# Transposing the gated sum, the convolution's operands and the compressed probabilities by VectorE blocks and DMAs in a decoder trunk

## The chip, the cores and the metric

The kernel runs on one core of a Trainium2 chip. A core has five engines with instruction queues of their own, which run in order: TensorE (PE in the profile: matmuls and transposes against an identity; PEld is its weight load), VectorE (DVE), ScalarE (ACT), GpSimd (POOL) and SyncE (SP). DMAs are issued from these queues and carried out by 16 DMA engines. The metric is the device time of one launch in microseconds (us), as a median of several runs; lower is better.

## The reference

Two layers of a hybrid decoder trunk on 256 tokens of width 1024, all in float32. Each layer is a half-step SwiGLU (2816 wide), a token mixer and a second SwiGLU, each between two RMSNorms:

```python
for l in range(2):
    x = x + 0.5 * rms_norm(swiglu(rms_norm(x, ...)), ...)
    x = x + rms_norm(token_mixer(rms_norm(x, ...), mem, ...), ...)
    x = x + 0.5 * rms_norm(swiglu(rms_norm(x, ...)), ...)
```

The mixer projects its input h once and splits the columns among three branches, whose outputs are gated and summed:

```python
u, bg, cg, q, kv, nsa_g, q_mem, merge_g = split(h @ w_in)
y_conv = bg * short_conv(cg * u, conv_w)               # 3 taps along the tokens, 512 channels
y_nsa  = nsa_attention(...)                            # compressed + selected blocks + window, 8 heads
y_mem  = cross_attention(q_mem, mem)                   # 4 heads, 256 memory tokens
merged = g_conv * (y_conv @ w_br_conv) + g_nsa * (y_nsa @ w_br_nsa) + g_mem * (y_mem @ w_br_mem)
return merged @ w_out
```

The compressed part of the attention has 15 compressed keys per group; its softmax gives 16 columns (one of them masked) for each of 8 heads, 128 columns for 128 tokens.

## The kernel before, in words

**Tiles.** The 256 tokens are two tiles of 128, t = 0 and 1, each a stream of work (`stream`, line 1451) that goes through the sub-layers of both layers in order. Every float32 matrix is split into a high and a low part of a reduced type (fp32r), and a product is three matmuls: high by high, high by low, low by high (`mm3`, line 395). Weights come from HBM by SP's queue into `raw`; `split_unit` (line 327) makes `whi` on ScalarE (line 333) and `wlo` on VectorE (line 334). One such unit serves both streams.

**Transposes.** A matmul contracts over partitions, so an operand that a stage leaves with tokens on partitions has to be turned before the next product. The kernel has two ways. `transpose4` (line 438) multiplies four 128x128 blocks by an identity on TensorE, into one of two PSUM banks `pt`; the users then read PSUM. `turn` (line 447) has VectorE transpose 32x32 blocks within each quarter of the partitions (tile `blocks`, line 451) and then four DMAs from GpSimd's queue carry the blocks to their partitions (tile `moved`, line 457), each DMA from a quarter of 32 partitions. For this, the source is written with its columns dealt out four apart (`lanes_in` reads with a stride of four floats, `lanes_out` writes runs of 32). `turn` is used for the SwiGLU gates, the memory, its keys and the probabilities of the selected, window and memory attention; `transpose4` for the rest.

**Order.** The program is written in steps: each `yield 0` of a stream is one step, usually six matmuls of 512 columns. The two streams take turns, stream 0 at most three steps ahead (`LEAD`), and other work (attention, compression, memory) runs in up to four lanes between the steps (`background`). `later(n, f)` puts f off by n steps: CONV, BS, PC, HALF and SECOND are such delays. Weight splits are written up to four steps ahead of their use (`AHEAD`). SP's queue keeps the written order; on the other engines a planner of the framework, which simulates the instructions with a cost model, fixes the order before the run, with priority by the written order. Small tiles of 520 columns come from one pool of eight (`TBUFS`, `ttile`), wide ones of 1024 from another (`gtile`), those of at most 128 columns from a third (`sp`).

**Around the change.** In `mixer` (line 1361) the projections u, C and B are made one after another. `conv_part` (line 1281) makes v = C * u, turns it, and applies the three taps with tokens along the free dimension, into `cT`; `conv_out` (line 1309) turns B into `bs`, multiplies and splits into `yconv`, which the first branch product reads. `cmp_attention` (line 1178) makes the compressed probabilities `pc` with a threefold copy, turns them with four 96-row transposes (line 1204) and splits them into `phc`. The branches follow in the order convolution, memory, sparse attention; each adds its gated half to `merged` (line 1438), and the two finished halves are turned by `transpose_half`, the first HALF = 5 steps after its last add, the second at step SECOND = 2 of the output product (`between`, line 1444). The output product (`output`, line 639) takes a pair of half products per step for k = 0 to 4; k from 4 up reads the second half.

## Time and profile before

| | |
|---|---|
| median of 3 runs | 1190.25 us (1189.96 to 1190.47) |
| the profiled execution | 1190.01 us, its span 1188.3 us |
| TensorE busy | 1177.2 us, 99%, 5777 matmuls, clock 0.999 of full |
| VectorE busy | 891.7 us, 75% |
| ScalarE busy | 755.9 us, 64% |
| GpSimd busy | 177.2 us, 15% |
| turns by blocks and DMAs | 44, with 176 DMAs of line 457, 4.3 us to landing in the median |
| transposes by `transpose4` (line 441) | 224 in all: x 96, qs 32, merged 32, qms 16, v 16, bs 16, kvs 8, kd 8 |
| transposes of pc (line 1204) | 16 |

The profile is one execution, followed by the hardware. In rows of groups a line reads: line of the kernel, engine, operation, tile written and tiles read, shapes, how many; then busy us, mean ns of one, and the engine's idle time ahead of them with what ended it. In rows by one line: min/median/max ns, first and last start. In a timeline: start, us, engine, line, operation. Matmuls are pipelined, so a matmul's record is longer than the time to the next one's start. The first layer's mixer runs from about 198 to 424 us, the second layer's from about 784 to 1010 us.

### The profile page before, as it was taken

To read this page: it belongs to the slowest core of one execution; us is meant where nothing else is said; L and a number is where in the kernel's file an instruction comes from. 1 tells how busy PE (TensorE), PEld (TensorE's weight loads), DVE (VectorE), ACT (ScalarE), POOL (GpSimd) and SP (SyncE) were. 2 spreads that over 40 slices of the span, in tenths; PEclk is the share of its full clock that TensorE was granted. 3 is DMA by queue.
4 is the path that set the end of the run, shared out by engine and by line. 5 is a ranking of instruction groups with operands and counts; after the bars stand their busy time and mean duration, and the time that the engine had idled before them with its cause. 6 is when DMAs were issued, how large, how long until landed. Compare 5 with 4: busy or idle time off the path is not lost.

```text
span 1188.3 us, 16619 instructions
## 1 busy us (share of the span) xinstructions
PE 1177.2 (99%) x5777; PEld 1032.5 (87%) x5777; DVE 891.7 (75%) x1130; ACT 755.9 (64%) x1217; POOL 177.2 (15%) x333
## 2 busy tenths in 40 slices
PE   9999999999999999999999999999999999999997
PEld 7888888888988888888888888889888888888886
DVE  6867757798998786676577677588899977767753
ACT  6655836888885565555465565469889655655541
POOL 4001301411120020011011011014012200110100
PEclk9999999999999999999999999999999999999999
DMA  7787875776678767777767678757767687587771
GB/s 258 253 256 240 276 261 154 228 240 192 194 231 216 247 185 221 222 235 230 228 184 230 215 229 270 240 141 242 232 178 229 198 231 229 178 250 213 234 223 63
DMA packets 133764, 260.64 MB, mean 219 GB/s; under 512 B 15694, under 2 KB 36848, under 8 KB 133680
## 3 DMA queue, kind: packets, MB, share of 16 engines
q1 hardware_dynamic: 124048, 235.11, 63.7%
q0 software_dynamic: 9600, 24.47, 7.6%
q8 instruction: 45, 0.74, 0.3%
q14 instruction: 39, 0.32, 0.1%
q10 hardware_dynamic: 32, 0.01, 0.0%
HBM read 235.42 MB, written 2.10 MB: 200 GB/s over the span
## 4 chain that ended last, share of the span: by engine, by line
PE 95%; ACT 2%; DVE 1%; issue 1%; DMA 0%; POOL 0%; SPq 0%; DVEq 0%; POOLq 0%; ACTq 0%
PE acc L410 35%; PE acc L396 9%; PE acc L397 9%; PE acc L398 9%; PE y L398 7%; PE y L396 7%; PE y L397 7%; PE pt L441 2%; PE br L396 2%; PE br L398 2%; PE br L397 2%; ACT whi L333 1%; PE s L1070 1%; DVE wlo L334 0%; PE om L1268 0%
## 5 line engine op out<-in xcount | busy, mean ns | idle before, releaser
L334 DVE TENSOR_TENSOR wlo<-raw,whi 128x1024 fp32r<-128x1024 f32 (+2 forms) x441 | 529.0, 1211 | 186.0 <-ACT whi L333 182.0
L333 ACT CAST whi<-raw 128x1024 fp32r<-128x1024 f32 (+2 forms) x441 | 452.6, 1040 | 255.2 <-PE acc L410 116.1
L457 POOL DMA_DIRECT2D moved<-blocks x176 | 95.8, 563 | 644.6 <-DVE blocks L451 368.9
L410 PE MATMUL acc<-wlo,hThi 128*128 128x512 f32 x640 | 191.6, 380 | 0.0
L410 PE MATMUL acc<-whi,hTlo 128*128 128x512 f32 x640 | 191.4, 380 | 0.0
L410 PE MATMUL acc<-whi,hThi 128*128 128x512 f32 x640 | 191.4, 381 | 0.0
L396 PE MATMUL acc<-whi,hThi 128*128 128x512 f32 (+1 forms) x480 | 182.8, 381 | 0.0
L397 PE MATMUL acc<-wlo,hThi 128*128 128x512 f32 (+1 forms) x480 | 179.3, 374 | 0.3 <-DVE wlo L334 0.2
L398 PE MATMUL acc<-whi,hTlo 128*128 128x512 f32 (+1 forms) x480 | 178.9, 373 | 0.0
L410 PEld LDWEIGHTS acc<-whi,hTlo 128*128 128x128 f32 x640 | 121.2, 189 | 17.3 <-DVE hTlo L513 0.4
L410 PEld LDWEIGHTS acc<-wlo,hThi 128*128 128x128 f32 x640 | 121.1, 189 | 17.0 <-DVE wlo L334 0.3
L410 PEld LDWEIGHTS acc<-whi,hThi 128*128 128x128 f32 x640 | 120.7, 189 | 16.6
L396 PE MATMUL y<-whi,turnhi 128*128 128x512 f32 x352 | 133.8, 380 | 0.0
L397 PE MATMUL y<-wlo,turnhi 128*128 128x512 f32 x352 | 133.7, 380 | 0.0
L398 PE MATMUL y<-whi,turnlo 128*128 128x512 f32 x352 | 133.7, 380 | 0.0
L398 PEld LDWEIGHTS acc<-whi,hTlo 128*128 128x128 f32 x480 | 90.9, 189 | 11.6
L397 PEld LDWEIGHTS acc<-wlo,hThi 128*128 128x128 f32 x480 | 91.1, 190 | 10.9 <-DVE wlo L334 0.9
L396 PEld LDWEIGHTS acc<-whi,hThi 128*128 128x128 f32 x480 | 91.1, 190 | 10.3
L398 PEld LDWEIGHTS y<-whi,turnlo 128*128 128x128 f32 x352 | 66.7, 189 | 9.2
L397 PEld LDWEIGHTS y<-wlo,turnhi 128*128 128x128 f32 x352 | 66.7, 189 | 9.2
L396 PEld LDWEIGHTS y<-whi,turnhi 128*128 128x128 f32 x352 | 66.7, 189 | 9.2
L475 DVE TENSOR_TENSOR turnlo<-moved,turnhi 128x1024 fp32r<-128x1024 f32 (+1 forms) x42 | 49.1, 1168 | 26.8 <-ACT turnhi L474 26.4
(307 smaller groups left out, 1449.6 us busy)
## 6 DMA issues: line engine op xcount, KB each, us to landing
raw<-in_ffn_w_in_dram SPq DMA_DIRECT2D x159, 512.0 KB, 4.7
raw<-in_w_mix_in_dram SPq DMA_DIRECT2D x96, 512.0 KB, 4.5
raw<-in_ffn_w_out_dram SPq DMA_DIRECT2D x88, 512.0 KB, 4.6
moved<-blocks POOLq DMA_DIRECT2D x144, 128.0 KB, 4.3
raw<-in_ffn_w_in_dram SPq DMA_DIRECT2D x34, 256.0 KB, 4.0
raw<-in_w_mem_kv_dram SPq DMA_DIRECT2D x16, 512.0 KB, 4.6
raw<-in_w_mix_out_dram SPq DMA_DIRECT2D x16, 512.0 KB, 4.9
raw<-in_cmp_k_w_dram SPq DMA_DIRECT2D x8, 512.0 KB, 4.6
```

The lines of the kernel that those rows point to most:

```text
L333: pinned(nc.scalar.copy(hi[:, c0:c1], raw[:, c0:c1]))
L334: pinned(nc.vector.tensor_sub(lo[:, c0:c1], raw[:, c0:c1], f32(hi[:, c0:c1])))
L396: nc.tensor.matmul(ps, lhsT=xh, rhs=wh, start=start, stop=False, skip_group_check=skip)
L397: nc.tensor.matmul(ps, lhsT=xh, rhs=wl, start=False, stop=False, skip_group_check=skip)
L398: nc.tensor.matmul(ps, lhsT=xl, rhs=wh, start=False, stop=stop, skip_group_check=skip)
L410: pinned(nc.tensor.matmul(ps[j][:, :n], lhsT=hT[x2][:, k], rhs=moving(w, j * n, n), start=(k == 0 and i == 0), stop=(k == 7 and i == 2)))
L441: pinned(nc.tensor.transpose(pt[:, j * P:(j + 1) * P], src[:, c0 + j * P:c0 + (j + 1) * P], ident))
L457: nc.gpsimd.dma_start(moved[0][:, q * f:(q + 1) * f], blocks[q * 32:(q + 1) * 32, :n].rearrange("j (p f) -> j p f", p=4))
L475: nc.vector.tensor_sub(lv, mv, f32(hv))
L1070: nc.tensor.matmul(s3[:, i], lhsT=QT[:, g * 2 + u, i], rhs=pairs(KT[j][:, var * 2 + g], 0, 256), start=(i == 0 and j == 0), stop=(i == 1 a ...
```

## The change

Four operands of the mixer no longer go through TensorE.

- v and bs are written dealt out four apart and turned by `turn` in place of `transpose4`, and the following instructions read the moved tile or `vT` in SBUF in place of PSUM. The scale of u and C is applied in one (`r[4]`, with `r[0]` for B in place of `r[1]`), so v is a plain product. The delays CONV and BS go from 7 and 4 to 9 and 9.
- pc is written once, without its copies, as 128 columns in a tile of the third pool; VectorE transposes its blocks, four DMAs bring the 32 columns of each pair of heads to partitions 0 to 31, and two ScalarE copies (one of them to partitions 64 to 95) and VectorE's subtraction make the three parts of `phc`. The delay PC of 3 after ATT_B becomes AWAY = 1 and PMOVED = 7.
- The last add of each half of merged writes `laned`, dealt out, which is turned by `turn`; the split comes 11 (first half) or 8 (second half) steps later, or at steps 0 and 4 of the output product if these come first. HALF and SECOND are no longer used.

```diff
--- before.py
+++ after.py
@@ -57,10 +57,12 @@
 LANES = 4
 NORM_B, NORM_C = 1, 1
 AWAY, SPLIT, RETURN = 1, 11, 6
+PMOVED = 7
+MOVED = {0: 11, 1: 8}
 MSTEP, MWAIT = (5, 11), 3
 ABREAST = 6
 SECOND_HALF = 1
-CONV, BS, CMP, ZC, QS_0, QS_1, QM, PC, YM = 7, 4, 6, 2, 2, 6, 2, 3, 1
+CONV, BS, CMP, ZC, QS_0, QS_1, QM, PC, YM = 9, 9, 6, 2, 2, 6, 2, 3, 1
 ATT_A, ATT_B, ATT_C, ATT_D, ATT_T = 1, 3, 2, 6, 8
 EARLY, RAMP, SCALES, STAGED, SETUP = 6, 10, 5, 8, 30
 DRAINED = 4
@@ -1194,17 +1196,21 @@
         sm = sp.tile([P, 8], F32, name="smc")
         nc.vector.tensor_reduce(sm, sc, axis=AX.X, op=OP.add)
         r = recip_gate(sm, 8, view(S["gt"][t], 0, [[3, 8]]))
-        pc = ttile("pc")
-        nc.vector.tensor_tensor(view(pc, 0, [[96, 4], [16, 2], [1, 16]]), view(sc, 0, [[16, 4], [64, 2], [1, 16]]),
+        pc = sp.tile([P, P], F32, name="pc")
+        nc.vector.tensor_tensor(view(pc, 0, [[32, 4], [16, 2], [1, 16]]), view(sc, 0, [[16, 4], [64, 2], [1, 16]]),
                                 view(r, 0, [[1, 4], [4, 2], [0, 16]]), op=OP.mult)
-        nc.scalar.copy(view(pc, 32, [[96, 4], [32, 2], [1, 32]]), view(pc, 0, [[96, 4], [0, 2], [1, 32]]))
-        yield ATT_B + PC
-        pt = tbank()
-        for i in range(4):
-            nc.tensor.transpose(pt[0:96, i * P:(i + 1) * P], pc[:, i * 96:(i + 1) * 96], ident)
+        blocks = sp.tile([P, P], F32, name="pb")
+        nc.vector.transpose(blocks, pc)
+        yield AWAY
+        moved = ttile("pmoved")
+        for q in range(4):
+            nc.gpsimd.dma_start(view(moved[0:32], q * 32, [[P, 4], [1, 32]]),
+                                view(blocks[q * 32:(q + 1) * 32], 0, [[32, 4], [1, 32]]))
+        yield PMOVED
         ph = ttile("phc", F32R)
-        nc.scalar.copy(ph[0:96, :512], pt[0:96])
-        nc.vector.tensor_sub(ph[32:64, :512], pt[32:64], f32(ph[32:64, :512]))
+        nc.scalar.copy(ph[0:32, :512], moved[0:32, :512])
+        nc.scalar.copy(ph[64:96, :512], moved[0:32, :512])
+        nc.vector.tensor_sub(ph[32:64, :512], moved[0:32, :512], f32(ph[0:32, :512]))
         yield ATT_D
         o = bank("oc")
         nc.tensor.matmul(o, lhsT=S["VST"][0:96], rhs=moving(ph[0:96], 0, 512), start=True, stop=True)
@@ -1281,44 +1287,42 @@
     def conv_part(t, l, u_s, c_ps, r):
         S = shared[l]
         v = ttile("v")
-        nc.vector.scalar_tensor_tensor(v[:, :512], c_ps, r[0], u_s[:, :512], op0=OP.mult, op1=OP.mult)
+        nc.vector.tensor_tensor(lanes_out(v, 0, [[P, 4]]), lanes_in(u_s, 0, 512), lanes_in(c_ps, 0, 512), op=OP.mult)
         cT = ttile("cT")
 
-        def turn():
-            pt = transpose4(v, 0)
+        def shifted(mv):
             vT = tp.tile([P, 4, 130], F32, name="vT", tag="tmp")
             if t == 0:
                 nc.gpsimd.memset(vT[:, :, 0:2], 0.0)
                 S["carry"] = sp.tile([P, 4, 2], F32, name="carry", bufs=1)
             else:
                 nc.gpsimd.tensor_copy(vT[:, :, 0:2], S["carry"])
-            nc.scalar.copy(vT[:, :, 2:130], pt.rearrange("p (c s) -> p c s", c=4))
+            nc.scalar.copy(view(vT, 2, [[130, 4], [32, 4], [1, 32]]), mv)
             if t == 0:
                 nc.gpsimd.tensor_copy(S["carry"], vT[:, :, 128:130])
             base = l * 48 + 32
             for c in range(4):
                 dst = cT[:, c * P:(c + 1) * P]
                 w = [convT[:, base + 4 * i + c:base + 4 * i + c + 1] for i in range(3)]
-                nc.scalar.activation(dst, pt[:, c * P:(c + 1) * P], AF.Copy, scale=w[2])
+                nc.scalar.activation(dst, vT[:, c, 2:130], AF.Copy, scale=w[2])
                 nc.vector.scalar_tensor_tensor(dst, vT[:, c, 1:129], w[1], dst, op0=OP.mult, op1=OP.add)
                 nc.vector.scalar_tensor_tensor(dst, vT[:, c, 0:128], w[0], dst, op0=OP.mult, op1=OP.add)
 
-        later(CONV, turn)
+        turn(v, 512, shifted, CONV)
         return cT
 
     def conv_out(cT, b_ps, r, put):
         bs = ttile("bs")
-        nc.scalar.activation(bs[:, :512], b_ps, AF.Copy, scale=r[1])
-
-        def turn():
-            pt = transpose4(bs, 0)
-            nc.vector.tensor_tensor(cT[:, :512], cT[:, :512], pt, op=OP.mult)
+        nc.scalar.activation(lanes_out(bs, 0, [[P, 4]]), lanes_in(b_ps, 0, 512), AF.Copy, scale=r[0])
+
+        def gated(mv):
+            nc.vector.tensor_tensor(quarters(cT[:, :512], 4), quarters(cT[:, :512], 4), mv, op=OP.mult)
             y = gtile("yconv", F32R)
             nc.scalar.copy(y[:, 0:512], cT[:, :512])
             nc.vector.tensor_sub(y[:, 512:1024], cT[:, :512], f32(y[:, 0:512]))
             put(y)
 
-        later(BS, turn)
+        turn(bs, 512, gated, BS)
 
     def branch(yT, name, l, n0):
         ps = bank("br")
@@ -1392,18 +1396,34 @@
         mem_query(t, l, ps, r)
         ps = yield from columns(0)
         u_s = ttile("us")
-        nc.scalar.activation(u_s[:, :512], ps, AF.Copy, scale=r[0])
+        nc.scalar.activation(u_s[:, :512], ps, AF.Copy, scale=r[4])
         ps = yield from columns(1024)
         cT = conv_part(t, l, u_s, ps, r)
         ps = yield from columns(512)
         made = []
         conv_out(cT, ps, r, made.append)
         merged = [ttile(f"merged{n}") for n in range(2)]
+        last_half = [None, None]
         mh, ml = gtile("mThi", F32R), gtile("mTlo", F32R)
 
         def transpose_half(n):
             sl = slice(n * 512, (n + 1) * 512)
             evac_split(mh[:, sl], ml[:, sl], transpose4(merged[n], 0))
+
+        placed = [False, False]
+
+        def move_half(n, laned, wait):
+            def place(mv):
+                if placed[n]:
+                    return
+                placed[n] = True
+                sl = slice(n * 512, (n + 1) * 512)
+                hv, lv = quarters(mh[:, sl], 4), quarters(ml[:, sl], 4)
+                nc.scalar.copy(hv, mv)
+                nc.vector.tensor_sub(lv, mv, f32(hv))
+
+            moved = turn(laned, 512, place, wait)
+            return lambda: place(turned_view(moved[0], 512))
 
         for b in ORDER:
             name = ("w_branch_conv", "w_branch_nsa", "w_branch_mem")[b]
@@ -1435,14 +1455,24 @@
                     nc.vector.scalar_tensor_tensor(dst, th[:, :512], 1.0, pb, op0=OP.add, op1=OP.mult)
                 else:
                     nc.vector.scalar_tensor_tensor(th[:, :512], th[:, :512], 1.0, pb, op0=OP.add, op1=OP.mult)
-                    nc.vector.tensor_add(dst, dst, th[:, :512])
-                if b == ORDER[2] and n == 0:
+                    if b == ORDER[2] and n in MOVED:
+                        laned = ttile("laned")
+                        nc.vector.tensor_tensor(lanes_out(laned, 0, [[P, 4]]), lanes_in(merged[n], 0, 512),
+                                                lanes_in(th, 0, 512), op=OP.add)
+                        last_half[n] = move_half(n, laned, MOVED[n])
+                    else:
+                        nc.vector.tensor_add(dst, dst, th[:, :512])
+                if b == ORDER[2] and n == 0 and 0 not in MOVED:
                     later(HALF, lambda: transpose_half(0))
         mT = tokens_last(mh, ml)
         y = [bank("y0"), bank("y1")]
 
         def between(k):
-            if k == SECOND:
+            if k == 0 and 0 in MOVED:
+                last_half[0]()
+            if k == 4 and 1 in MOVED:
+                last_half[1]()
+            if k == SECOND and 1 not in MOVED:
                 transpose_half(1)
 
         yield from output(y, "w_mix_out", l, 8, lambda k: (mT[0][:, k], mT[1][:, k]), between)
```

`turn`, `lanes_in`, `lanes_out`, `turned_view` and `quarters` are those of the kernel before.

## The prediction

> **What bounds the kernel now.** I read the page first, for the busy shares and the chain of work that ended last.
>
> ```profile
> span 1188.3 us, 16619 instructions
> PE 1177.2 (99%) x5777; PEld 1032.5 (87%) x5777; DVE 891.7 (75%) x1130; ACT 755.9 (64%) x1217; POOL 177.2 (15%) x333
> ...
> PE 95%; ACT 2%; DVE 1%; issue 1%; DMA 0%; POOL 0%; SPq 0%; DVEq 0%; POOLq 0%; ACTq 0%
> ```
>
> TensorE sets the end almost everywhere, so work taken from it is worth its issue time, as long as no other engine makes it wait instead. Next came the windows of the first mixer, because a share of 75% for VectorE is a mean over unlike stages. A row gives the stretch and its length, then the busy us (and instructions) of PE, PEld, DVE, ACT and POOL, the clock, the DMA share and GB/s.
>
> ```profile
> 278.00:294.00 16.00, 16.00 (x92) 14.24 (x91) 15.27 (x34) 12.85 (x26) 2.66 (x7) 1.00 0.70 233
> 294.00:310.00 16.00, 16.00 (x92) 14.39 (x91) 15.06 (x26) 12.27 (x32) 2.18 (x4) 1.00 0.52 144
> 310.00:326.00 16.00, 16.00 (x89) 14.42 (x89) 15.01 (x23) 16.00 (x41) 2.16 (x4) 1.00 0.77 230
> 326.00:342.00 16.00, 16.00 (x80) 14.04 (x79) 15.55 (x22) 13.19 (x27) 4.34 (x8) 1.00 0.80 252
> 342.00:358.00 16.00, 16.00 (x80) 13.94 (x79) 15.61 (x25) 13.22 (x29) 2.16 (x4) 1.00 0.73 214
> 358.00:374.00 16.00, 16.00 (x76) 13.93 (x75) 13.31 (x14) 8.58 (x12) 2.17 (x4) 1.00 0.79 212
> ...
> 390.00:406.00 16.00, 16.00 (x80) 14.05 (x79) 12.97 (x15) 9.57 (x12) 0.00 (x0) 1.00 0.80 260
> ```
>
> From 278 to 358 us, where the convolution and the compressed attention run, VectorE is busy 76.5 of 80 us: it is nearly a second bound. From 358 on it has about 3 us free in 16. The third view counts, for the weights' low parts (tile wlo), the VectorE splits begun and the TensorE matmuls that used them, from the start of the span to a given time (columns PE, PEld, DVE). Each split serves four matmuls (441 splits, 1760 uses), so splits less a quarter of the uses says how far VectorE is ahead.
>
> ```profile
> 0.00:252.00 252.00, 128.74 (x388) 71.10 (x388) 117.66 (x100) 1.00 0.76 240
> ...
> 0.00:342.00 342.00, 170.75 (x500) 92.17 (x501) 151.40 (x128) 1.00 0.74 233
> 0.00:358.00 358.00, 178.66 (x521) 96.04 (x521) 158.66 (x134) 1.00 0.74 232
> ...
> 0.00:408.00 408.00, 206.05 (x594) 109.87 (x594) 183.85 (x155) 1.00 0.75 232
> ```
>
> The lead is 100 - 388/4 = 3.0 splits at 252 us, 3.0 at 342, 3.75 at 358 and 6.5 at 408. At 251 us TensorE does wait for a split, as the waits of TensorE and the chain show:
>
> ```profile
> PE z L1111 <- DVE wlo L334: 1.0, 2, 0.6
> ```
> ```profile
> 250.99 0.30 PE z L1111
> ```
>
> So in the convolution's stage VectorE has about one split in hand, and in the stage of the gated sum (from about 382 us) three more.
>
> **What TensorE is rid of.** Five groups of four transposes per token tile and layer: v, bs, pc and the two halves of merged.
>
> ```profile
> L441 PE MATMUL pt<-ident,merged x32: 272/273/273, 389.0 to 997.0; 128*128 128x128 f32 x32
> ...
> L441 PE MATMUL pt<-ident,v x16: 271/273/275, 288.5 to 883.0; 128*128 128x128 f32 x16
> ...
> L441 PE MATMUL pt<-ident,bs x16: 272/273/273, 297.4 to 892.8; 128*128 128x128 f32 x16
> ```
> ```profile
> L1204 PE MATMUL pt<-ident,pc x16: 272/273/273, 286.1 to 878.9; 128*96 128x128 f32 x16
> ```
> ```profile
> 388.76 0.38 PE L398 MATMUL acc<-whi,hTlo 128*128 128x512 f32 x1
> 388.97 0.60 PE L441 MATMUL pt<-ident,merged 128*128 128x128 f32 x4
> 389.33 0.46 PE L396 MATMUL acc<-whi,hThi 128*128 128x512 f32 x1
> 389.63 0.38 PE L397 MATMUL acc<-wlo,hThi 128*128 128x512 f32 x1
> ```
>
> The 273 ns of a record is latency; what counts is start to start. A wide matmul takes 0.215 us to the next start (388.76 to 388.97). From 388.76 to 389.63 stand two wide matmuls and a group in 0.87 us, so a group costs 0.44 us. 80 transposes are 20 groups: 8.8 us. Per layer (two token tiles) that is 2.64 us in the convolution's stage and 1.76 us in the gated sum's. Nothing else leaves TensorE.
>
> **What VectorE gets.** The rows nearest to the new instructions:
>
> ```profile
> L451 DVE STREAM_TRANSPOSE blocks<-wide 128x1024 f32<-128x1024 f32 x16 | 19.8, 1239 | 0.0
> ...
> L1438 DVE TENSOR_TENSOR merged<-merged,gth 128x512 f32<-128x512 f32 x16 | 10.9, 684 | 0.3
> ...
> L451 DVE STREAM_TRANSPOSE blocks<-wide 128x768 f32<-128x768 f32 x8 | 7.8, 975 | 0.1
> ...
> L573 DVE TENSOR_TENSOR hf<-pt,gT 128x256 f32<-128x256 f32 x20 | 7.5, 417 | 0.0
> ...
> L1095 DVE TENSOR_TENSOR F<-G,smallT 128x240 f32<-128x240 f32 x8 | 4.2, 572 | 0.1
> ...
> L1284 DVE SCALAR_TENSOR_TENSOR v<-acc,rs,us 128x512 f32<-128x512 f32 x4 | 3.0, 746 | 0.0
> ```
> ```profile
> L333 ACT CAST whi<-raw 128x1024 fp32r<-128x1024 f32 x431 | 446.4, 1049 | 255.1 <-PE acc L410 116.1 <-PE y L398 67.5 <-PE acc L398 34.4
> ...
> L816 ACT COPY mp<-m 128x1024 f32<-128x1024 f32 x2 | 5.9, 2949 | 0.0
> ```
>
> The line through 1024 and 768 columns gives a block transpose of 0.71 us for 512 columns and 0.31 for 128 (bounds: 0.15, in proportion, and 0.98). The product v and the last add now read SBUF with a stride of four floats (lanes_in). Their nearest rows are apart. Line 816 reads SBUF on ScalarE by that very pattern, 2949 ns against 1049 for a plain cast: 0.95 us more for 512 columns. Line 1095 on VectorE reads one strided operand, 572 ns for 240 columns where 256 plain ones take 417: 0.36 us more for 512. The lower bound is nothing. I take VectorE's own row for v, which has one such operand in SBUF (1.05 us, 0.3 more than 746), and a value between the two rows for the add, which has two (1.3, 0.6 more than 684).
>
> The Trainium skill, SBUF — State Buffer, section Door 1: The DMA port swizzle, says that SBUF is read in lines of 16 bytes, that an access which crosses to a new line pays, and that four fp32 is as far as one strides for free. By that last clause the stride here is free, and the sum below would be 3.2 us lower: 1.2 for v, and 2.0 for the second halves, which would then be in time. Line 816 has this stride and is 2.8 times as long, so I go by the row.
>
> Per layer the convolution's stage gets 2 x (2 x 0.71 + 0.31 + 0.3) = 4.1 us more of VectorE, and has 2.64 x 0.95 = 2.5 us less in which to do it, 6.6 us in all. What covers it: half of the 3.5 us that VectorE idles from 278 to 358 (the other half are waits within chains), 1.75; the one split in hand, 1.2; and what can slide past 358, where 2.7 us are free, 2.0. That is 4.95, so TensorE waits 1.7 us and keeps 0.9 of its 2.64. The bounds are 2.64 kept (all covered) and 4.0 lost (nothing covered, 6.6 us of waits against 2.64).
>
> The gated sum's stage gets 4 x (0.71 + 0.6) = 5.2 us of VectorE per layer, covered by the 3 us in 16 and three splits. There the question is lateness, not load.
>
> **The late second half.** Rows of VectorE's and TensorE's timelines around the first token tile's last add and its output product, then of an earlier turn, of the DMAs' line and of the cast:
>
> ```profile
> 399.56 0.68 DVE L1438 TENSOR_TENSOR merged<-merged,gth 128x512 f32<-128x512 f32 x1
> ```
> ```profile
> 409.71 0.38 PE L396 MATMUL y<-whi,mThi 128*128 128x512 f32 x1
> ```
> ```profile
> 272.39 1.25 DVE L451 STREAM_TRANSPOSE blocks<-p 128x1024 f32<-128x1024 f32 x1 [1.10 <-ACT p L1055]
> ...
> 274.24 2.22 POOL L457 DMA_DIRECT2D moved<-blocks  x4 [29.01 <-DVE vst L1171]
> ```
> ```profile
> L457 POOL DMA_DIRECT2D moved<-blocks x176: 541/559/607, 52.6 to 1133.4; - x176
> ...
> DMA to landing us min/median/max: 2.5/4.3/5.9
> ```
> ```profile
> L432 ACT CAST mThi<-pt 128x512 fp32r<-128x512 f32 x8 | 4.7, 586 | 6.9 <-PE pt L441 6.9
> ```
>
> The product's fifth pair, the first that reads this half, starts at 409.71, and at 409.3 without the group ahead of it: 9.7 us after the add. The new way takes 1.3 (add), 0.71 (blocks), 0.6 (from the blocks' end at 273.64 to the first issue at 274.24), 1.65 (three more issues), 4.3 (landing; pieces are half as large, so perhaps a little less) and 0.6 (the cast on ScalarE): 9.2 us. That leaves 0.5 us, and the cast and the subtraction can each stand behind a weight split (1.05 and 1.22 us) in queues that run in order, and behind them the next splits. I take 0.5 us late per tile (bounds 0 and 2.0), 1.0 per layer; of 1.76 us 0.76 is kept. The first half has the second half's gates and branch still ahead, six steps of its own stream or 7.8 us more, and is free; without that cover it would cost the same 0.5.
>
> **What costs nothing.** GpSimd issues 80 more DMAs at 0.56 us, 45 us in all; behind a DMA that waits for its blocks stand the carry copy, the memset of vT and the attention's own DMAs. It is busy at most 4.3 of 16 us above, and CONV and BS now leave nine planner steps (six matmuls, 1.3 us each), so the cover is 11.7 us; without it the first of these would cost a landing, 4.3. ScalarE loses the copy and the 96-row cast of pc and gets two 32-row casts, 0.2 us more per tile, under the same steps. SP's queue is not touched.
>
> **The sum.** 2 x (0.9 + 0.76) = 3.3 us off the profiled execution. It took 1190.0 (span 1188.3 and 1.7 around it); the median of the runs is 1190.25. So 1186.8 for the median, 0.29% faster.
>
> **The rivals.**
> - VectorE keeps up: all 8.8 us stay, 1181.4. For it: over the span it is idle a quarter, and nine steps of delay let the splits go first. Against it: 95% busy for 80 us on end, with a lead that sinks to the 3.0 at which TensorE waited.
> - VectorE becomes the bound of 278 to 358 us (and of its like in layer 2). From the point at which the covers fall under 4.0 us, the stage is longer than before; with none it loses 4.0 per layer instead of keeping 0.9, 9.8 us more: 1196.6. For it: strided reads may cost as line 816's do. Against it: the work can slide.
> - The second halves are 2.0 us late in place of 0.5, four times: 6 us more, 1192.8. The gain of that stage is gone at 0.9 late. For it: four more links in queues that run in order. Against it: DMAs that land in under 4.3.
> - Tiles run short: each turn holds two of the eight "tmp" tiles over a landing. If an evacuation waits for one, half a landing a layer is lost, 4.3 us: 1191.1. No row shows such a wait before.
>
> **How the numbers follow.** A measurement of this kernel tells about 0.2%, 2.4 us, from no change. Forecast 0.42, its own range 1184 to 1189, so faster 0.31 and same 0.11. Keeps up 0.22, faster. VectorE the bound 0.14, slower. Late halves 0.15, same 0.07 and slower 0.08. Tiles short 0.07, same 0.04 and slower 0.03. Together 0.53, 0.22 and 0.25. The range 1180.8 to 1194.5 leaves out the far half of the VectorE case and the edges.
>
> **What would show it.** TensorE 80 matmuls fewer, VectorE's transposes near 0.71 and 0.31 us, the add near 1.3: right in size. TensorE waiting for wlo between 278 and 358: the forecast's loss. If 278 to 358 shrinks by 2.6 us with no such wait, VectorE keeps up and I am wrong. TensorE waiting for mThi or mTlo (lines 432 and 433 in the old numbering) shows the late halves; waits of ScalarE or GpSimd ahead of a first write to a tmp tile show the shortage.

## The result and the profile after

The changed kernel takes 1200.3 us (median of 4 runs, 1197.75 to 1203.06) against 1190.36 for the kernel before: a ratio of 1.0084, 95% interval 1.0062 to 1.0107. It is 9.9 us slower, where 3.4 us faster was predicted; the time lies above the range's upper end of 1194.5 us. The profiled execution took 1197.75 us. Line numbers of helpers are two higher than before (`wlo` is L336, the DMAs of `turn` L459).

The page of the changed kernel, its first lines and the chain by engine:

```profile
span 1196.0 us, 16672 instructions
...
PE 1173.7 (98%) x5697; PEld 1024.1 (86%) x5697; DVE 910.7 (76%) x1150; ACT 758.8 (63%) x1217; POOL 218.8 (18%) x413
...
PE 77%; DVE 7%; ACT 6%; DMA 5%; issue 3%; POOL 2%; SPq 0%; DVEq 0%; POOLq 0%; ACTq 0%
```

The 80 transposes are gone, and the chain that ended last runs through TensorE for 77% of its length, where it was 95%. The rest is mostly VectorE, ScalarE and DMAs. In this execution TensorE stands still for 22.3 us of the span (1196.0 - 1173.7), against 11.1 before. It is busy only 3.5 us less, although 8.8 us of work were taken from it, so the matmuls that are left took some 5.3 us longer; the last section comes back to this. The waits of TensorE name the places (total us, times, longest):

```profile
PE y L398 <- ACT mThi L1422: 5.8, 2, 2.9
PE om L1274 <- ACT bs L1316: 2.5, 2, 2.4
PE pt L443 <- DMA x<-in_x_dram: 2.4, 1, 2.4
...
PE z L1113 <- DVE wlo L336: 1.0, 2, 0.6
PE s L1072 <- ACT p L973: 0.8, 1, 0.8
PE s L1072 <- ACT gth L1435: 0.7, 2, 0.4
```

The wait for `x` stands at the start of the span and varies from run to run; in this execution it makes 1 us more than in that of before. New are the output product waiting for the second half of merged, 2.9 us in each layer, and `om` waiting for the copy of `bs`. There is no new wait for `wlo`.

The new VectorE instructions, by groups (busy, mean ns of one):

```profile
L1290 DVE TENSOR_TENSOR v<-us,acc 128x512 f32<-128x512 f32 x4 | 6.0, 1506 | 0.0
L1460 DVE TENSOR_TENSOR laned<-merged,gth 128x512 f32<-128x512 f32 x8 | 12.7, 1584 | 0.1
L453 DVE STREAM_TRANSPOSE blocks<-laned 128x512 f32<-128x512 f32 x8 | 5.7, 709 | 0.2
L453 DVE STREAM_TRANSPOSE blocks<-v 128x512 f32<-128x512 f32 x4 | 2.8, 708 | 0.0
```

**The convolution's stage.** Its window before, and after (columns as in the prediction):

```profile
278.00:358.00 80.00, 80.00 (x425) 71.03 (x424) 76.50 (x125) 67.53 (x149) 13.51 (x27) 1.00 0.71 214
```
```profile
278.00:358.00 80.00, 76.47 (x389) 65.87 (x389) 76.18 (x123) 66.50 (x140) 26.55 (x52) 1.00 0.73 213
```

VectorE is as busy as it was, 76 us of 80, and gets through no more: with the new work on top the stage takes longer. ScalarE's rows suggest how that reaches TensorE. In the timeline of the changed kernel (last column: idle before, and what ended it):

```profile
282.97 0.31 ACT L1195 ACTIVATE sc<-sc 128x128 f32<-128x128 f32 x1 [3.01 <-DVE sc L1194]
...
292.76 0.31 ACT L1195 ACTIVATE sc<-sc 128x128 f32<-128x128 f32 x1 [1.73 <-DVE sc L1194]
...
295.89 0.47 ACT L1254 ACTIVATE pm<-sm,nmm 128x256 f32<-128x256 f32 x1 [1.89 <-DVE nmm L1251]
...
300.55 0.69 ACT L1316 ACTIVATE bs<-acc,rs 128x512 f32<-128x512 f32 x1
...
309.11 0.69 ACT L1316 ACTIVATE bs<-acc,rs 128x512 f32<-128x512 f32 x1
...
309.84 0.38 PE L1274 MATMUL om<-turnhi,vm 128*128 128x256 f32 x1 [2.35 <-ACT bs L1316]
```

and the same two copies of the kernel before:

```profile
290.67 0.72 ACT L1311 ACTIVATE bs<-acc,rs 128x512 f32<-128x512 f32 x1
...
301.52 0.68 ACT L1311 ACTIVATE bs<-acc,rs 128x512 f32<-128x512 f32 x1
```

From 280 to 296 us ScalarE waits 6.6 us for three small VectorE results and then has a backlog. The copies of `bs` come 9.9 and 7.6 us later than before (some 2 us of that stand already ahead of the stage); until then B stays in its PSUM bank, and `om` waits for the second copy.

These rows alone do not show that ScalarE's waits are the cause. From 270 to 345 us ScalarE waits 8.8 us for VectorE, and 8.1 us in the kernel before, where the waits lie elsewhere. The kernel with only the probabilities and the first half of merged moved (1188.13 us, below) waits for the same results and makes the same copies 7.4 and 3.0 us later than before, yet TensorE has no wait in this stretch:

```profile
282.33 0.31 ACT L1195 ACTIVATE sc<-sc 128x128 f32<-128x128 f32 x1 [2.78 <-DVE sc L1194]
...
292.75 0.47 ACT L1254 ACTIVATE pm<-sm,nmm 128x256 f32<-128x256 f32 x1 [1.87 <-DVE nmm L1251]
...
298.10 0.73 ACT L1317 ACTIVATE bs<-acc,rs 128x512 f32<-128x512 f32 x1
...
304.56 0.70 ACT L1317 ACTIVATE bs<-acc,rs 128x512 f32<-128x512 f32 x1
```

**The second half.** The first token tile's, in the timeline of the changed kernel:

```profile
404.76 1.58 DVE L1460 TENSOR_TENSOR laned<-merged,gth 128x512 f32<-128x512 f32 x1
...
406.37 0.71 DVE L453 STREAM_TRANSPOSE blocks<-laned 128x512 f32<-128x512 f32 x1
...
407.64 2.16 POOL L459 DMA_DIRECT2D moved<-blocks  x4 [9.04 <-DVE blocks L453]
...
412.80 0.38 PE L400 MATMUL y<-whi,mTlo 128*128 128x512 f32 x1
...
415.37 0.62 ACT L1422 CAST mThi<-moved 128x512 fp32r<-128x512 f32 x1 [4.77 <-DMA moved<-blocks]
...
416.04 0.48 PE L398 MATMUL y<-whi,mThi 128*128 128x512 f32 x1 [2.87 <-ACT mThi L1422]
```

From the add to the product it takes 11.3 us; TensorE would have been ready at 413.0, 8.3 us after the add. The four DMAs, looked at alone, land 2.2, 2.5, 4.3 and 5.8 us after their issues, in this order:

```profile
DMA to landing us min/median/max: 2.2/3.4/5.8
```

### The profile page after: what moved, and what is told of

Same layout as the page of the kernel before. It is cut to its first block, busy times and chain, and to the rows that moved or that the text cites. A ratio compares the mean times of both kernels' runs of the same rounds, so it can differ in the third digit from the quotient of the medians.

```text
span 1196.0 us, 16672 instructions
## 1 busy us (share of the span) xinstructions
PE 1173.7 (98%) x5697; PEld 1024.1 (86%) x5697; DVE 910.7 (76%) x1150; ACT 758.8 (63%) x1217; POOL 218.8 (18%) x413
## 4 chain that ended last, share of the span: by engine, by line
PE 77%; DVE 7%; ACT 6%; DMA 5%; issue 3%; POOL 2%; SPq 0%; DVEq 0%; POOLq 0%; ACTq 0%
PE acc L412 35%; PE y L400 6%; PE y L398 6%; PE y L399 6%; PE acc L399 6%; PE acc L398 6%; PE acc L400 6%; DMA moved<-blocks 3%; DVE wlo L336 3%; ACT whi L335 2%; POOL moved L459 1%; PE pt L443 1%; PE br L398 1%; PE br L400 1%; PE br L399 1%
## 5 line engine op out<-in xcount | busy, mean ns | idle before, releaser
L336 DVE TENSOR_TENSOR wlo<-raw,whi 128x1024 fp32r<-128x1024 f32 (+2 forms) x441 | 528.3, 1210 | 169.0 <-ACT whi L335 166.0
L459 POOL DMA_DIRECT2D moved<-blocks x240 | 130.4, 564 | 691.8 <-DVE blocks L453 361.6
L398 PEld LDWEIGHTS acc<-whi,hThi 128*128 128x128 f32 x480 | 91.0, 190 | 10.8 <-ACT p L973 0.2
```

The costliest lines, as they stand in the source:

```text
L336: pinned(nc.vector.tensor_sub(lo[:, c0:c1], raw[:, c0:c1], f32(hi[:, c0:c1])))
L398: nc.tensor.matmul(ps, lhsT=xh, rhs=wh, start=start, stop=False, skip_group_check=skip)
L459: nc.gpsimd.dma_start(moved[0][:, q * f:(q + 1) * f], blocks[q * 32:(q + 1) * 32, :n].rearrange("j (p f) -> j p f", p=4))
```

## The experiments

The theory after the result: in the convolution's stage VectorE has no room, ScalarE falls behind it and holds PSUM banks, and the second halves are late by the length of their path. Its first part is the load theory of the expectations. Rivals: the strided reads, too few tiles, the deeper steps, or the DMAs themselves. All runs are timed against the kernel before, which stood at 1190.15 to 1190.31. The intervals behind the ratios are about 1 us to either side for most runs, and up to 2.7 us for the changed kernel, so a difference of two experiments is uncertain by 1 to 3 us.

### The parts alone

```diff
 # sum only: conv_part, conv_out, cmp_attention, CONV, BS as before
-MOVED = {0: 11, 1: 8}            # convolution only, probabilities only
+MOVED = {}                       # and the other part as before
```

Merged alone:

> Only the gated sum's halves are moved; the convolution and the compressed probabilities go through TensorE as before. TensorE is rid of 8 groups, 3.5 us. Theory 'strided reads and late halves' (the last adds take 1.58 us, the second halves come 3 us late, once per layer): waits for mThi of about 3 us in each layer stay, and the time is 1190.4 - 3.5 + 6 and some slow matmuls after each wait, near 1194. Rival 'only the parts together' (too much VectorE work at once, too few tiles): alone this part has room, no wait for mThi over 1 us, and the time is near 1187.

The convolution's v and bs alone:

> Only v and bs are moved. TensorE is rid of 8 groups, 3.5 us. Theory 'strided reads and late halves': v still takes 1.5 us of VectorE, ScalarE falls behind it and holds PSUM banks; waits of 2 to 4 us in the first layer, near 1190. Rival 'only the parts together': near 1187, no wait for bs.

The probabilities alone:

> Only the compressed probabilities are moved. TensorE is rid of 4 groups, 1.8 us; VectorE gets 4 transposes of 0.31 us. Both theories: near 1189, and no new wait. If it is slower than before, the DMAs by themselves cost something.

Measured: 1190.94 us (ratio 1.0005, 0.9996 to 1.0014), 1193.54 (1.0029, 1.0017 to 1.0040) and 1189.5 (0.9995, 0.9986 to 1.0004). The differences add up to +3.5 us, the whole has +9.9: the parts make each other dearer. Only the probabilities came out as expected, near 1189. Merged alone lies between its two theories (near 1194, near 1187), and the convolution alone is slower than both of its (near 1190, near 1187). Merged alone already shows its wait, only shorter, and the convolution alone has waits of its own kind:

```profile
PE y L398 <- ACT mThi L1420: 3.1, 2, 1.7
```
```profile
PE om L1270 <- ACT yf L1030: 2.2, 1, 2.2
...
PE s L1042 <- ACT bs L1312: 1.2, 1, 1.2
```

### The whole without strided reads, by another row order

```diff
-RUNS = {..., "w_branch_conv": 64, ...}     # rows of the weight per partition run
+RUNS = {..., "w_branch_conv": 16, ...}     # w_mix_out 16 too
-   nc.vector.tensor_tensor(lanes_out(laned, ...), lanes_in(merged[n], ...), lanes_in(th, ...), op=OP.add)
+   nc.vector.tensor_add(laned[:, :512], merged[n][:, :512], th[:, :512])
```

> The whole change, but v, bs and the last sum are written in their own order and the dealing out is done by the order in which the rows of w_branch_conv, w_mix_out and the taps are loaded (runs of 16 in place of 64), so nothing on VectorE reads with a stride. Theory 'strided reads': v falls from 1.52 to about 0.7 us and the last add from 1.58 to 0.69, the second halves come 0.9 us earlier, VectorE has 3.5 us less per layer in the convolution's and the sum's stages together, and of the 18.7 us that the change lost against its 8.8 us of TensorE work at least 8 come back: 1192 or less. Rival 'landings and tiles': the waits for mThi and of the DMAs for tiles stay, 1197 to 1200.

Measured 1202.66 us (1.0110, 1.0093 to 1.0127). It is slower than both theories allowed. The adds are short, but TensorE's waits for mThi are 8.3 us in place of 5.8. The run says little of strided reads, since it changed something else too: a load of w_mix_out lands in 6.5 us, where it took 4.9 in the kernel before and 4.6 in the changed one, and the stage of the gated sum shows a DMA share of 0.97, for 0.76 and 0.88. That the other row order of the weights is dearer to fetch is likely, and was not tried alone:

```profile
384.00:420.00 36.00, 31.61 (x134) 26.84 (x132) 25.86 (x30) 17.87 (x20) 8.66 (x16) 0.91 0.97 252
```

### More tiles

```diff
-GBUFS = 21
-TBUFS = 8
+GBUFS = 20
+TBUFS = 10
```

> The whole change, with ten tmp tiles in place of eight (and one of the large tiles fewer). Tiles-run-short theory: GpSimd's wait ahead of the second token tile's second half (7.5 us in the changed kernel, for VectorE's mTlo) goes, the late copy of bs too, and TensorE's waits for mThi and bs fall under 2 us together: 1196 us or less. Theory of late second halves and a full VectorE and ScalarE in the convolution's stage: GpSimd's wait goes, but TensorE still waits about 5 us for mThi and about 2 us for bs, as the first token tile's second half waits for no tile: 1199 to 1202 us.

Measured 1200.19 us (1.0071, 1.0054 to 1.0088). GpSimd's wait for mTlo is gone, and so is the wait of `om` for bs (in its place `om` waits 1.1 us for another tile). But the waits for mThi are 7.5 us in place of 5.8, and the time is the same within its interval. So tiles may have had a part in the wait for bs, but more of them do not win back the loss.

### The second half back on TensorE

```diff
-MOVED = {0: 11, 1: 8}
+MOVED = {0: 11}
```

> The whole change, with the second half of merged transposed by TensorE as before; the first half, v, bs and the probabilities are moved. TensorE gets 4 groups back, 1.8 us. Theory of late second halves: the waits for mThi (5.8 us) and the slow matmuls behind them go: 1195 to 1197 us, and what is left above 1190 belongs to the convolution's stage (om waiting for bs stays near 2.5 us). Rival, that the convolution's stage alone makes the loss and the second halves' waits only take up its time: 1199 us or more.

Measured 1195.4 us (1.0038, 1.0027 to 1.0049): the second halves make 4.9 us of the loss, though they free 4 groups of transposes. The wait for mThi is gone and the convolution's stands as it was:

```profile
PE om L1274 <- ACT bs L1316: 2.5, 2, 2.4
```

### The dealing done by ScalarE

```diff
-   nc.scalar.activation(u_s[:, :512], ps, AF.Copy, scale=r[4])
+   nc.scalar.activation(lanes_out(u_s, 0, [[P, 4]]), lanes_in(ps, 0, 512), AF.Copy, scale=r[4])
 # the last gates likewise; merged by a ScalarE copy after the second branch
```

> The whole change, but ScalarE puts the elements in the dealt order (u_s and the last branch's gates as they leave PSUM, the sum before the last branch by a copy), so that VectorE reads nothing in SBUF at a 16-byte stride; weights and row orders stay those of the changed kernel. VectorE is rid of about 0.8 us in each of 12 instructions, some 10 us; ScalarE gets about 10 us more. Theory that the strided reads on VectorE make the loss: 1193 us or less, TensorE's waits for mThi under 2 us. Theory that landing and load make it: the second half's add ends 0.9 us earlier and the wait for mThi falls by about that much per layer, from 2.9 to 2 us each, and ScalarE, being fuller, gives some of it back: 1197 to 1201 us.

Measured 1197.3 us (1.0050, 1.0035 to 1.0065). Every VectorE read is contiguous and 3.0 of the 9.9 us are gone, which is what the theory of landing and load gave; the waits for mThi are 1.8 and 1.7 us.

### Only probabilities and first half

```diff
 # after, with conv_part, conv_out, CONV and BS as before
-MOVED = {0: 11, 1: 8}
+MOVED = {0: 11}
```

> Only the probabilities and the first half of merged are moved; v, bs and the second half stay on TensorE. TensorE is rid of 8 groups, 3.5 us. Theory that a part without a late landing keeps its groups: 1187 to 1188.5 us, no new wait of TensorE. Rival, that each moved turn gives its groups back in load on VectorE and the DMA engines even where nothing waits for it: 1189.5 to 1191 us, as probabilities alone gave 0.7 of their 1.8 us.

Measured 1188.13 us (0.9978, 0.9969 to 0.9987): faster than before, with no new wait over 0.6 us. Of the 3.5 us freed it keeps 2.2. On this base the convolution's parts can be priced singly.

### VectorE's load alone

```diff
+   for _ in range(2):                          # after v
+       nc.vector.transpose(spare, v[:, :480])
+   nc.vector.transpose(spare, bs[:, :480])     # after bs
```

> The kernel before, with three more block transposes of 480 columns on VectorE per token tile and layer (two of v, one of bs, about 0.66 us each, their output used by nothing) at the places where the changed kernel has its new VectorE work; nothing is moved, TensorE keeps all its transposes. Per layer that is 4.0 us more of VectorE. Load theory (a full VectorE makes ScalarE late, which holds PSUM banks back): 1194 to 1199 us, with waits of TensorE for om, s or bs between 290 and 330 us. Rival, that the moves themselves make the loss (landings waited for, steps nine deep that change the order of the work): 1192 us or less.

Measured 1192.27 us (1.0017, 1.0008 to 1.0027). VectorE load alone costs 2.0 us; the load theory had asked for 4 or more, the rival for 1192 or less. Load is a cause, but not the only one. And it acts here in another way than the theory says: the copies of bs start at 291.22 and 299.72 us, about as early as before, TensorE does not wait for om, s or bs, and its new waits are for wlo and hTlo, about 1 us each.

### bs alone, v alone, and v without the strided product

```diff
 # on top of probabilities and first half: conv_out as in after (bs),
 # or conv_part as in after (v), or that and u_s dealt by ScalarE (v dealt)
+   nc.scalar.activation(lanes_out(u_s, 0, [[P, 4]]), lanes_in(ps, 0, 512), AF.Copy, scale=r[4])
```

> Probabilities and first half moved, as in the kernel of 1188.1 us, and bs as well; v stays on TensorE. TensorE is rid of 4 more groups, 1.8 us; VectorE gets 0.7 us per token tile. Load theory: little VectorE work, so 1187 to 1190 us. Rival, that the late copy of bs and its landing are the cause: 1191.5 us or more, with om waiting for bs about 2 us.

> Probabilities and first half moved, and v as well; bs stays on TensorE. VectorE gets 1.5 us per token tile (0.8 for the strided product, 0.7 for the blocks). Load theory: most of the convolution's loss is here, 1191 to 1195 us. Rival that bs is the cause: 1187 to 1189 us.

> As the run with v moved, but ScalarE writes u_s in the dealt order as it leaves PSUM, so that VectorE's product reads SBUF contiguously and is 0.8 us shorter; the blocks stay. Load theory: 1.5 to 3 us less than the run with v moved. Rival, that v's landing or its nine steps make the loss: within 1 us of that run.

Measured 1191.09 us with bs (1.0005, 0.9995 to 1.0014), 1189.64 with v (0.9994, 0.9985 to 1.0004) and 1187.65 with v dealt (0.9974, 0.9965 to 0.9984). Against the base of 1188.13, bs costs 3.0, v 1.5, and v dealt changes nothing that can be told (0.5 less). The two single costs add up to 4.5 us; both together, 1195.4, cost 7.3. The first two times lie between their two theories, so neither is confirmed. The expectation that most of the loss is v's fell: bs, with less VectorE work, costs more. The rival's wait of `om` for bs did not come either. With bs, the longest new wait of TensorE inside the layers is for a sum of VectorE in the attention, not for the landing:

```profile
PE oc L1216 <- DVE yf L1013: 1.6, 1, 1.6
```

The last comparison changes one thing only: one operand, read contiguously, is worth 2.0 us (1189.64 to 1187.65). In the group of v with u_s dealt:

```profile
L1290 DVE TENSOR_TENSOR v<-us,acc 128x512 f32<-128x512 f32 x4 | 2.7, 678 | 0.0
```

### The nine steps alone

```diff
-CONV, BS, ... = 7, 4, ...
+CONV, BS, ... = 9, 9, ...        # in the kernel before
```

> The kernel before with nine planner steps in place of seven and four between v or bs and its transposes by TensorE; nothing is moved. Theory that the deeper delay makes a good part of the convolution's loss (it changes the order in VectorE's and ScalarE's queues): 1192 us or more. Load or latency theory: 1189.5 to 1191 us.

Measured 1190.14 us (0.9997, 0.9988 to 1.0007): the steps alone, without moves, cost nothing.

### The convolution's taps left out, and their control

```diff
-   nc.vector.scalar_tensor_tensor(dst, vT[:, c, 1:129], w[1], dst, op0=OP.mult, op1=OP.add)
-   nc.vector.scalar_tensor_tensor(dst, vT[:, c, 0:128], w[0], dst, op0=OP.mult, op1=OP.add)
```

> The kernel with probabilities, v, bs and first half moved (1195.4 us), with the convolution's two multiply-adds per channel group on VectorE left out (16 instructions per layer and some 4.2 us of VectorE; the convolution then has one tap of three). All moves, landings and steps stay. Load theory: VectorE's cover is back, 1185 to 1189 us, and TensorE's wait of om for bs goes. Latency or order theory: 1192 us or more, with that wait still there.

> The kernel before with the same multiply-adds left out, the control of the run without them: 1189 to 1190.5 us, as TensorE sets the end and waits little for VectorE there. If it is under 1188 us, the gain of the other run is partly that of a shorter chain and not of the cover.

Measured 1192.28 us (1.0016, 1.0007 to 1.0026) and, for the control, 1190.66 (1.0003, 0.9993 to 1.0012). Taking some 8.6 us off VectorE over both layers (904.4 to 895.8 us of busy time) takes 3.1 us off the 1195.4, and nothing off the kernel before. The result is split: the wait of `om` for `bs` is gone, as the load theory says, but the time is the one that the latency or order theory gave, 1192 or more, and other waits stand in its place:

```profile
PE br L399 <- DVE wlo L336: 1.3, 2, 0.7
...
PE oc L1216 <- ACT p L973: 0.9, 1, 0.9
PE br L398 <- ACT whi L335: 0.9, 2, 0.6
```

### v and bs moved, without the strided product

```diff
 # the run of 1195.4 us, with u_s dealt by ScalarE as above
```

> Probabilities, v, bs and first half moved, with u_s dealt by ScalarE as it leaves PSUM, so that VectorE's product is 0.8 us shorter, 1.6 us per layer. Load theory with a threshold: more than twice 1.6 us falls away, 1190 to 1192.5 us. Latency or order theory: 1194 us or more.

Measured 1191.5 us (1.0010, 1.0000 to 1.0020): some 3.3 us less VectorE work over both layers (904.4 to 901.1) is worth 3.9 us. That is inside what load with a threshold gave, and outside the other theory. Here the traces follow the chain by way of ScalarE: its waits for the small sums `sc` in the first layer fall from 5.5 to 3.2 us, the copies of bs start at 297.38 and 305.94 us in place of 298.40 and 306.96, and the wait of `om` falls from 2.4 to 1.6 us. But work taken off ahead of these sums is worth more than the larger amount taken off at the taps, behind the first copy. So where the work stands seems to count as much as how much it is.

### Moves whose results nothing reads

```diff
+   beside(v, 512, lambda mv: None, 9)      # turn(), in the kernel before
+   beside(bs, 512, lambda mv: None, 9)
```

> The kernel before, TensorE keeping all its transposes, with the block transposes of v and bs on VectorE (0.7 us each, 2.8 us per layer) and their four DMAs each issued besides, into tiles that nothing reads. Theory that the moves as such cost (GpSimd's queue, the DMA engines, tiles): 1193.5 us or more, as VectorE load alone gave 2.0 for 4.0 us per layer. Theory that only load and the waiting for results cost: 1190.3 to 1192 us.

Measured 1193.33 us (1.0025, 1.0016 to 1.0035), between the two theories: with less VectorE work than the run of load alone it costs 3.1 in place of 2.0 us, so the moves as such cost about 1 us. The largest new wait is for VectorE:

```profile
301.47 0.66 PE L441 MATMUL pt<-ident,bs 128*128 128x128 f32 x4 [1.14 <-DVE phc L1209]
```

### The second half's DMAs from two queues

```diff
-   nc.gpsimd.dma_start(moved[0][:, q * f:(q + 1) * f], ...)
+   (nc.scalar if both and q > 1 else nc.gpsimd).dma_start(moved[0][:, q * f:(q + 1) * f], ...)
```

> The whole change, with two of the second half's four DMAs issued by ScalarE's queue beside GpSimd's two, so that the last issue comes about 1.1 us earlier. Theory that the path is too long by its links: TensorE's waits for mThi fall from 2.9 to about 1.8 us each, 1197.5 to 1199.5 us. Theory that full DMA engines set the landing: the waits stay at 2.5 us or more, 1199.5 to 1202 us.

Measured 1197.62 us (1.0063, 1.0047 to 1.0079), 2.7 less than the change. The issues, and the landing of these four:

```profile
404.50 0.71 DVE L453 STREAM_TRANSPOSE blocks<-laned 128x512 f32<-128x512 f32 x1
...
405.30 1.34 ACTq L459 DMA_DIRECT2D moved<-blocks  x2
...
405.76 1.08 POOL L459 DMA_DIRECT2D moved<-blocks  x2 [9.04 <-DVE blocks L453]
...
410.11 0.61 ACT L1422 CAST mThi<-moved 128x512 fp32r<-128x512 f32 x1
```
```profile
DMA to landing us min/median/max: 2.6/3.1/3.4
```

From the end of the blocks (405.21) to the cast it takes 4.9 us, where the change takes 8.3 (407.08 to 415.37), and TensorE hardly waits for mThi (0.3 us in all). What is late next is its low part: VectorE subtracts it only after the second token tile's strided add.

```profile
PE y L400 <- DVE mTlo L1423: 2.8, 2, 1.5
```
```profile
1000.00 1.10 DVE L1460 TENSOR_TENSOR laned<-merged,gth 128x512 f32<-128x512 f32 x1
1001.03 0.68 DVE L1423 TENSOR_TENSOR mTlo<-moved,mThi 128x512 fp32r<-128x512 f32 x1
...
1001.76 0.48 PE L400 MATMUL y<-whi,mTlo 128*128 128x512 f32 x1 [1.51 <-DVE mTlo L1423]
```

So the path was too long by its links, the landing of four DMAs in a row among them, and VectorE's queue is the next limit.

## Why the prediction was wrong

**What TensorE is rid of.** Right: 80 matmuls fewer, and where nothing comes late, most of the time freed is kept (2.2 of 3.5 us with probabilities and first half).

**Durations.** The blocks were right (0.71 us). VectorE's busy time rose by 19.0 us (891.7 to 910.7), near the 2 x (4.1 + 5.2) = 18.6 that the forecast's terms add up to. That is partly luck: records that overlap count once, and the strided reads were put too low: v took 1.51 us for the 1.05 forecast, the add 1.58 for 1.3. Line 816's row was the nearer for both, and on VectorE one strided operand in SBUF costs nearly as much as two (0.83 us more than 0.68, and 0.90). The clause of the Trainium skill (SBUF — State Buffer, Door 1: The DMA port swizzle) that four fp32 are strided for free disagrees with these rows, and with the 0.68 us of v when its operand in SBUF is dealt beforehand.

**The convolution's stage.** This step failed in sign. It took 6.6 us of VectorE work per layer against 4.95 of cover, and had 0.9 per layer left. The probabilities alone change nothing that can be told, and v and bs, on the base of probabilities and first half, cost 1195.4 - 1188.1 = 7.3 us. The count of the cover knew one deadline only, the weights' low parts, and took the rest of the work to slide. In the changed kernel it did not slide: TensorE waited for bs (2.5 us) and for the attention's tiles, not for wlo, and the stage lost time where it was to gain some. The reading of the traces is that ScalarE takes its queue in order and waits for VectorE's small results, and that behind these stand the copies that free PSUM banks. The run without the strided product bears it out in part; the load run, in which the copies came on time and TensorE waited for wlo and hTlo, and the kernel of 1188.13 us, whose copies came late without harm, show that it is not the whole cause. The rival "VectorE becomes the bound", 9.8 us above the forecast, had the place and nearly the price, though its price was that of VectorE's own work and not of a wait for bs.

Of these 7.3 us, 10.8 with the 3.5 that TensorE was freed of, the strided product makes 3.9 (1195.4 to 1191.5). Moves that nothing reads cost 3.1, measured on the kernel before, 2.0 or less of it VectorE's load. The steps make nothing. The remaining 3.8 or so (10.8 - 3.9 - 3.1, across two bases, each difference uncertain by 1 to 2 us) was not separated: later results and a lower clock behind the waits are candidates, and neither is shown.

**The late second half.** The direction was right, the size not: 0.5 us was taken, 2.9 measured in each layer's first token tile. Two terms were off. The path was 11.3 us for 9.2: add 0.3 more, and from the first issue to the cast 7.7 for 1.65 + 4.3 = 5.95. The 4.3 was the median landing of single DMAs; what counts is the last of four, and that took 5.8. The time allowed was 8.3 us for 9.7. With merged moved alone it is 9.7, as forecast (398.62 to 408.3 us in the first layer), and the path is as long, 11.3 us; the waits are 3.1 us in both layers for 5.8 in the whole change. So the shorter time comes with the other parts, most likely because VectorE runs later against TensorE after the convolution's stage. The second token tile's half, with the same price in the forecast, caused no wait. Put back on TensorE, the second halves give 4.9 us: 5.8 of waits less the 1.8 freed are 4.0 of it. The rest, 0.9, is within the uncertainty.

**Tiles.** GpSimd did wait for a tile, 7.5 us by its waits; two more tiles removed that and won nothing that can be told. The rival was rightly small, though more tiles removed the wait of `om` for bs as well.

**The chances.** Two rivals came true at once. Each had been priced as if the rest went by the forecast; with both, 1186.8 + 9.8 + 6.0 = 1202.6 us, which the range's upper end of 1194.5 left out, as it did the first rival's 1196.6 alone. That this sum is near the measured 1200.3 is partly luck: two waits of 2.9 us stand where it has four of 2.0. The rivals were not independent: with the convolution's operands and the probabilities moved too, the waits for the second halves grow from 3.1 to 5.8 us.

**A better version.** Probabilities, first half and v moved, with u_s dealt as it leaves PSUM, takes 1187.65 us, 0.26% less than the kernel before. It cannot be told from the kernel without v (1188.13).

## What to carry to other kernels

An engine that is 95% busy through a stage can be a second bound, and its slack is not what it idles: ask which queues wait on its small results, and what these queues hold (here PSUM banks). A hand-over by several DMAs ends with the last landing, so price it by the maximum of a group and not by the median of one. Parts of a change that draw on the same slack have to be priced together, and tried apart: here a part of the change is a gain and the whole a loss.

## What the runs showed of the hardware

- **A stride of 16 bytes.** VectorE takes 1506 ns for 512 columns when one SBUF operand is read four floats apart, and 678 when only the operand in PSUM is; ScalarE's copy of bs out of PSUM at that stride takes 0.69 us, as without it (0.68 and 0.72).
- **DMAs in a row.** The four issued from GpSimd's queue at 0.56 us each land in 2.2 to 5.8 us; shared by two queues, in 2.6 to 3.4, at the same DMA share. The row of the changed kernel and of the one with two queues:

```profile
407.00:413.00 6.00, 6.00 (x29) 5.08 (x27) 6.00 (x7) 1.84 (x2) 2.16 (x4) 1.00 0.84 258
```
```profile
405.00:411.00 6.00, 6.00 (x29) 5.25 (x28) 3.98 (x5) 4.25 (x6) 1.08 (x2) 1.00 0.84 269
```

  The Trainium skill, DMA: Bandwidth & Descriptors, section Issuing engines are not separate DMA queues, says that issuing from several engines saves only the time to initiate. Here two issues fewer in a row are 1.1 us, and the way from blocks to cast is 3.4 us shorter. Why the rest is saved, no run here shows: the two stretches differ in more than the queue, as VectorE is busy 6.00 of 6 us in the first and 3.98 in the second.
- **The clock after a pause.** After TensorE's pause of 3.2 us in the run with more tiles the granted clock was 0.50 for 3.5 us, and after one of 1.8 us in the run with ScalarE's dealing too; after the change's pause of 2.9 us, in the profiled execution, it stayed at 1.00. The rows of the first two runs:

```profile
413.50:417.00 3.50, 3.50 (x9) 2.73 (x9) 3.24 (x4) 2.60 (x3) 2.17 (x4) 0.50 0.71 228
417.00:420.00 3.00, 3.00 (x11) 2.41 (x10) 0.82 (x2) 1.05 (x1) 0.01 (x1) 0.68 0.90 291
```
```profile
413.00:415.50 2.50, 2.50 (x7) 2.02 (x6) 1.54 (x2) 1.50 (x2) 0.54 (x1) 0.50 0.85 252
```

  In the run with more tiles that is 0.5 x 3.5 + 0.32 x 3 = 2.7 us for one pause. The four runs of the changed kernel had mean clocks of 0.997, 0.994, 0.996 and 0.994 at 1197.75, 1203.06, 1199.91 and 1200.69 us. The same 2.4 us wait of `om` for bs is followed by a clock of 0.55 and 0.54 over 309 to 312 us in the kernel of 1195.4 us and in the one with two queues, and by 1.00 in the changed kernel's profiled execution. So a wait can cost more than its length, and not the same in every run. As an estimate, a mean clock of 0.994 in place of the 0.999 before is 6 us over a span of 1190 us, about half of what the two slowest of the four executions lost; 0.997 is 2.4 us, part of the 5.3 us by which the matmuls of the profiled execution took longer. No trace shows where the slower executions lost it.
